# Gates of the merge ahead of its projections, a head in 128-row pieces behind products of zeros, and a last output block in halves

## The chip, the cores and the metric

The kernel runs on one core of a Trainium2 chip. The metric is the device time of one execution in microseconds (us), as a median of repeated runs. Before the change it is 2555.0 us (2554.29 to 2555.2 in 3 runs). One further execution was profiled; all times of single instructions come from it.

## The reference

One block of a hybrid network on 256 tokens with 2048 features, in fp32: a gated feed-forward layer, a mixer with two recurrent branches, cross-attention over a memory of 256 tokens, a second feed-forward layer, and a last norm.

```python
h = rmsnorm(x, norm_ffn1)
x = x + 0.5 * ((silu(h @ w1) * (h @ w3)) @ w2)
h = rmsnorm(x, norm_mix)
(mq, mk, mv, mo, mi, mf, hq, hf, hi, hg, gate_m, gate_h) = split(h @ w_in)
y_m = mlstm_mixer(mq, mk, mv, mo, mi, mf, ...)      # 4 heads
y_h = hgrn2_mixer(hq, hf, hi, hg, ...)              # 8 heads
merged = sigmoid(gate_m) * (y_m @ w_proj_m) + sigmoid(gate_h) * (y_h @ w_proj_h)
x = x + merged @ w_out
x = x + cross_attention(rmsnorm(x), rmsnorm(mem), w_q, w_kv, w_o)
x = x + 0.5 * swiglu(rmsnorm(x), ...)
return rmsnorm(x, norm_final)
```

## The kernel before

**Products.** Every large product goes through `gemm_nat`. It makes a block of 2 x 128 tokens by 512 columns (344 for three of the mixer's), in two PSUM banks `pa`. The activations stand still and the weights stream. Each fp32 operand is split into a high and a low part (activations `oh`, `ol`; weights `wh`, `wl`), and for each 128 rows of weights and each token half three products are made: high x high (L248), high x low (L249), low x high (L250). Weights come in units of 512 rows (1 MB, tile `wr`, four buffers, DMAs on SP). Each unit is worked off in two steps called subs, of 2 x 128 rows and 12 products each. For each sub ScalarE (ACT) makes `wh` by a cast and VectorE (DVE) makes `wl` by a subtraction, three subs ahead of the products (`SPLIT_AHEAD`).

**Order of the work.** `self.steps` is one list of subs and functions for the whole block, and `run` goes through it. After each sub `tick` adds the sub's modelled duration to a clock `self.pe`. Pieces of other work wait in two lists: `timed` (after so many ticks) and `bg` (in order). `tick` issues pieces while the modelled end of DVE's and ACT's queues, kept by `Paced` from a base and a price per element, is less than `BACKLOG` = 2.0 us ahead. All engines take their queues in order; within limits the framework's scheduler also reorders independent instructions when the program is built. `written(p)` runs timed pieces until an operand that a product needs has been issued; `flush` empties both lists.

**The head.** `load_x` (L425) orders the DMAs on SP: two halves of the first quarter of x, the first unit of weights in two halves, then quarters of x and units in turn. `first` transposes the first quarter on TensorE (PE), eight 128x128 pieces into two banks (L277), and splits them with the norm's gain. The first sub follows.

**The mixer and its merge.** The recurrent branches' work stands in `bg`: `hgrn_levels`, `hgrn_out`, `mlstm_weights`, `mlstm_scores`, `mlstm_out`. Their results are transposed by DVE in 16 steps of 32x256 (`tt<-mo`) into operand pairs `self.Y`. The merge loops over four column blocks c: gate `gm`, gate `gh`, `y_h @ w_proj_h`, `y_m @ w_proj_m`. After the gates of c = 0 stands a `flush()`.

**The end.** The last block (c = 3 of the second `w2`) runs with `late=4`: the products of token half 1 of its last 8 x 128 rows are put behind those of half 0, so that half 0 is finished, normed and written meanwhile. `done_last` then does for each half: add to x, squares on ACT, sum, `rstd` on GpSimd (POOL, L447), product with the gain, scaling, four DMAs.

Of the kernel before, what the change touches and what calls it, by code (L numbers as in the profile page):

```python
# [19 lines left out]
P = 128  # L20
# [79 lines left out]
class Core:  # L100
    def __init__(self, nc):
        self.tensor, self.gpsimd, self.sync = nc.tensor, nc.gpsimd, nc.sync
        self.vector, self.scalar = Paced(nc.vector, 0.13, 0.00106), Paced(nc.scalar, 0.22, 0.00082)


class Block:
# [74 lines left out]

    def flush(self):
        while self.timed or self.bg:
            if self.timed:
                self.next_timed()
            else:
                self.bg.popleft()()
# [9 lines left out]
    def split(self, s):  # L197
# [8 lines left out]
        self.nc.scalar.copy(s.hi, raw)  # L206
        self.nc.vector.tensor_sub(s.lo, raw, s.hi.bitcast(F32))
# [17 lines left out]


    def gemm_nat(self, ops, wap, n0, n, evac, kts=None, row0=0, late=0):
# [6 lines left out]
        def mm_for(k0, nk):  # L234
            def mm(hi, lo, ts=(0, 1)):
                if k0 == 0:
                    box["ps"] = [self.pacc([P, n]) for _ in range(2)]
                if k0 >= nkt - 2 * late and len(ts) == 2:
                    ts = (0,)
                    box.setdefault("late", []).append(lambda: mm(hi, lo, (1,)))  # L240
                for j in range(nk):
                    kt = k0 + j
                    xh, xl = self.written(pairs[kt // 4])
                    for t in ts:
# [5 lines left out]
                        nc.tensor.matmul(o, a_l, hi[:, j, :], start=False, stop=(kt == nkt - 1))  # L250
            return mm

        for k0 in range(0, nkt, 4):
            u = Unit(wap, row0 + k0 * P, 4, n0, n, 2)
            for q in range(2):
                self.steps.append(Sub(u, q, mm_for(k0 + 2 * q, 2)))
# [4 lines left out]
        def finish():  # L261
# [3 lines left out]
            evac(box["ps"], (1,))  # L265
        self.do(finish)

    def turn(self, src, gain, dst, halves=(0, 1)):
# [3 lines left out]
        for h in halves:  # L272
            ps = self.ps([P, 2, T])
            for j in range(2):
                for t in range(2):
                    c = (2 * h + j) * P
                    nc.tensor.transpose(ps[:, j, t * P:(t + 1) * P], src(t)[:, c:c + P], self.ident)  # L277
# [3 lines left out]
            else:  # L281
                for j in range(2):
                    k = 2 * h + j
                    g = gain[:, k:k + 1]
                    nc.scalar.activation(hi[:, k, :], ps[:, j, :], AF.Copy, scale=g)
                    nc.vector.scalar_tensor_tensor(
                        lo[:, k, :], in0=ps[:, j, :], scalar=g, in1=hi[:, k, :].bitcast(F32),
                        op0=ALU.mult, op1=ALU.subtract)
            if h == 1:
                self.unwritten.pop(id(dst), None)  # L290

# [5 lines left out]
    def written(self, p):  # L297

        while id(p) in self.unwritten:
            self.next_timed()  # L300
        return p
# [44 lines left out]
    def setup(self):  # L346
# [21 lines left out]
        def load(group):  # L368
            st = self.const.tile([P, P], F32, name=self.nm("stage"))
            first = group[0][1]  # L370
            for name, o, n in group:
# [3 lines left out]
                nc.scalar.dma_start(st[o - first:o - first + n, :], src.rearrange("(k p) -> k p", p=P))  # L375
# [8 lines left out]

        nc.scalar.dma_start(self.ident, a["consts"][:, :P])
        turn_first = load(groups[0])
        nc.vector.memset(self.mhalf, -0.5)

        def rest():
            nc.scalar.dma_start(c[:, P:], a["consts"][:, P:])  # L390
            turns = [load(g) for g in groups[1:]]
            self.gbias = self.const.tile([P, 8], F32, name="gbias")
            nc.scalar.dma_start(self.gbias[:, 0:4], a["mlstm_ig_bias"][0].partition_broadcast(P))
            nc.scalar.dma_start(self.gbias[:, 4:8], a["mlstm_fg_bias"][0].partition_broadcast(P))
# [8 lines left out]
        return turn_first  # L403

# [37 lines left out]
    def rstd_of(self, ss, n, dim):  # L442
# [4 lines left out]
        nc.gpsimd.tensor_tensor(r, ms, self.mhalf[:, :n], op=ALU.pow)  # L447
        return r

    def squares(self, src, ss_col):  # L450
        junk = self.t2([P, 512], name="junk")
        self.nc.scalar.activation(junk[:, :src.shape[-1]], src, AF.Square, accum_out=ss_col)
# [22 lines left out]
    def squares_of(self, n, c):  # L475
        for t in range(2):
            self.squares(self.x[c][:, t, :], n.ss[:, t, c:c + 1])
# [17 lines left out]
    def ffn(self, norm, w1, w3, w2, chunk_done, end=False):  # L495
        nc = self.nc
        ops = LazyOps(lambda: norm().ops)
        for f0, f1 in ((0, 6), (6, 11)):
            us = [None] * (f1 - f0)
            for f in range(f0, f1):  # L500
# [16 lines left out]
                self.gemm_nat(ops, w1, f * 512, 512, evac_a)  # L517
                self.gemm_nat(ops, w3, f * 512, 512, evac_b)
            for c in range(4):
                last = f1 == 11  # L520

                def evac(ps, ts=(0, 1), c=c, last=last):
# [7 lines left out]
    def mixer(self, norm, chunk_done):  # L530
# [83 lines left out]
        merged = [None] * 4  # L614
        G = {}
        for c in range(4):
# [560 lines left out]
```

## Time and profile before

| | us |
|---|---|
| median of 3 runs | 2555.0 |
| the profiled execution, time of the run | 2555.04 |
| its span, first to last instruction | 2553.2 |
| outside the span | 1.84 |
| first PE instruction | 4.84 |
| first large product | 10.00 |
| last large product starts | 2544.05 |

Page part 1 gives the busy time of each engine; matmuls overlap in it, so that a busy PE says little. What counts is the step from one product to the next: the rows of the timeline show a product as 0.39 us long, but the next one starts 0.23 us later. The waits name what PE stood still for. The gates of c = 0 begin about 1090 us into the span.

### The profile page before, as it was taken

How to read it: one execution, taken by the hardware profiler on the slowest of the kernel's cores; microseconds unless marked ns; L12 is line 12 of the kernel's file. 1: busy time of each engine (PE TensorE's matmuls, PEld its weight loads, DVE VectorE, ACT ScalarE, POOL GpSimd, SP SyncE). 2: the span in 40 equal slices, each digit the busy share in tenths (PEclk: the TensorE clock that was granted, in tenths of full speed). 3: DMA queues.
4: the chain of work that ended last, by engine and by line, in shares of the span. 5: the costliest groups of instructions: out<-in, count | busy, mean ns of one | idle time of the engine just before them, and what ended most of it. 6: DMA issues, size and time to landing. Idle time of an engine off the chain costs nothing.

```text
span 2553.2 us, 29044 instructions
## 1 busy us (share of the span) xinstructions
PE 2528.8 (99%) x11431; PEld 2104.7 (82%) x11431; DVE 1730.7 (68%) x2384; ACT 1201.8 (47%) x1385; POOL 13.5 (1%) x21
## 2 busy tenths in 40 slices
PE   8999999999999999999999999999999999999998
PEld 7888888888888898787888888888888888888887
DVE  5767644767768878967666787677767574457664
ACT  5444434444455565644444454444544443344443
POOL 0000000000000000000000000000000000000000
PEclk9999999999999999999999999999999999999999
DMA  7665565565555545545555565555566556555653
GB/s 262 197 193 189 195 198 190 189 198 190 193 190 185 176 138 165 183 163 181 190 191 197 187 212 180 170 175 173 190 198 190 191 196 197 188 192 194 214 189 128
DMA packets 243305, 479.92 MB, mean 188 GB/s; under 512 B 8008, under 2 KB 14432, under 8 KB 243168
## 3 DMA queue, kind: packets, MB, share of 16 engines
q1 hardware_dynamic: 242016, 476.15, 57.4%
q10 hardware_dynamic: 1152, 1.92, 0.2%
q8 instruction: 89, 1.46, 0.2%
q14 instruction: 48, 0.39, 0.0%
HBM read 475.94 MB, written 2.10 MB: 187 GB/s over the span
## 4 chain that ended last, share of the span: by engine, by line
PE 92%; DVE 6%; issue 1%; ACT 0%; DMA 0%; POOL 0%; SPq 0%; POOLq 0%; ACTq 0%
PE pa L250 30%; PE pa L248 30%; PE pa L249 30%; DVE wl L90 2%; DVE tt L90 2%; PE ps L726 1%; DVE ol L90 1%; DVE cv L90 0%; PE ps L277 0%; DMA x<-in_x 0%; PE ps L966 0%; PE ps L967 0%; PE ps L965 0%; POOL rstd L447 0%; ACT kn L90 0%
## 5 line engine op out<-in xcount | busy, mean ns | idle before, releaser
L90 DVE TENSOR_TENSOR wl<-wr,wh 128x1024 fp32r<-128x1024 f32 (+1 forms) x904 | 1094.2, 1213 | 721.6 <-ACT wh L90 715.0
L90 ACT CAST wh<-wr 128x1024 fp32r<-128x1024 f32 (+1 forms) x904 | 942.0, 1045 | 1141.9 <-PE pa L250 1091.3
L248 PE MATMUL pa<-wh,oh 128*128 128x512 f32 (+1 forms) x3616 | 1409.7, 390 | 7.0 <-ACT oh L90 4.4
L249 PE MATMUL pa<-wl,oh 128*128 128x512 f32 (+1 forms) x3616 | 1403.6, 388 | 2.3 <-DVE wl L90 2.3
L250 PE MATMUL pa<-wh,ol 128*128 128x512 f32 (+1 forms) x3616 | 1402.5, 388 | 0.2 <-DVE ol L90 0.2
L248 PEld LDWEIGHTS pa<-wh,oh 128*128 128x128 f32 x3616 | 680.0, 188 | 143.3 <-ACT oh L90 4.8
L249 PEld LDWEIGHTS pa<-wl,oh 128*128 128x128 f32 x3616 | 680.2, 188 | 141.1 <-DVE wl L90 5.5
L250 PEld LDWEIGHTS pa<-wh,ol 128*128 128x128 f32 x3616 | 679.7, 188 | 138.8 <-DVE ol L90 0.7
L90 DVE STREAM_TRANSPOSE tt<-sil 32x256 f32<-32x256 f32 x352 | 153.6, 436 | 6.8
L90 DVE STREAM_TRANSPOSE tt<-x 32x256 f32<-32x256 f32 x144 | 62.8, 436 | 2.8
L90 ACT CAST oh<-tt 128x1024 fp32r<-128x1024 f32 x29 | 30.6, 1054 | 39.7 <-DVE tt L90 39.7
L90 ACT ACT_TABLE_LOAD x34 | 43.6, 1283 | 10.1 <-DVE rs L90 3.1
L90 ACT ACTIVATE oh<-tt,cols 128x256 fp32r<-128x256 f32 x52 | 23.3, 500 | 47.7 <-DVE tt L90 47.7
L90 ACT ACTIVATE sil<-pa,rstd 128x512 f32<-128x512 f32 x44 | 29.8, 689 | 17.8 <-PE pa L250 17.7
L90 DVE TENSOR_TENSOR ol<-tt,oh 128x1024 fp32r<-128x1024 f32 x29 | 35.4, 1220 | 1.6 <-ACT oh L90 1.4
L90 DVE STREAM_TRANSPOSE tt<-kn 32x256 f32<-32x256 f32 x64 | 27.9, 436 | 5.6 <-ACT kn L90 4.5
L90 DVE SCALAR_TENSOR_TENSOR sil<-pa,rstd,sil 128x512 f32<-128x512 f32 x44 | 31.0, 743 | 0.0
L90 DVE STREAM_TRANSPOSE qt<-qn 32x256 f32<-32x256 f32 x64 | 27.9, 436 | 4.1 <-ACT qn L90 3.0
L90 ACT ACTIVATE oh<-ps,cols 128x256 fp32r<-128x256 f32 x44 | 20.3, 473 | 21.4 <-DVE ol L90 15.6
L90 DVE COPY_PREDICATED at<-cst,ps 128x128 f32<-128x128 int32 x80 | 22.8, 328 | 10.6 <-PE ps L726 10.0
L90 ACT ACTIVATE junk<-x 128x512 f32<-128x512 f32 x40 | 24.9, 625 | 7.6 <-DVE x L90 7.0
L90 DVE SCALAR_TENSOR_TENSOR ol<-ps,cols,oh 128x256 fp32r<-128x256 f32 x44 | 20.7, 480 | 10.8 <-ACT oh L90 10.5
(174 smaller groups left out, 649.4 us busy)
## 6 DMA issues: line engine op xcount, KB each, us to landing
wr<-in_ffn_w SPq DMA_DIRECT2D x263, 1024.0 KB, 5.2
wr<-in_w_in SPq DMA_DIRECT2D x80, 1024.0 KB, 5.1
wr<-in_xattn_wkv SPq DMA_DIRECT2D x32, 1024.0 KB, 5.4
wr<-in_w_out SPq DMA_DIRECT2D x16, 1024.0 KB, 5.1
wr<-in_xattn_wq SPq DMA_DIRECT2D x16, 1024.0 KB, 5.0
wr<-in_xattn_wo SPq DMA_DIRECT2D x16, 1024.0 KB, 5.1
wr<-in_w_in SPq DMA_DIRECT2D x12, 688.0 KB, 4.1
wr<-in_w_proj_h SPq DMA_DIRECT2D x8, 1024.0 KB, 5.0
```

The lines of the kernel that those rows point to most:

```text
L90: return fn(out, *args, **kw)
L248: nc.tensor.matmul(o, a_h, hi[:, j, :], start=(kt == 0), stop=False)
L249: nc.tensor.matmul(o, a_h, lo[:, j, :], start=False, stop=False)
L250: nc.tensor.matmul(o, a_l, hi[:, j, :], start=False, stop=(kt == nkt - 1))
L726: nc.tensor.matmul(ps[:, i, :], kt[:, g, j * P:(j + 1) * P], S["qc"][:, 2 * g + j, :], start=True, stop=True)
```

## The change

It has five parts.

1. **Merge.** The gates of c = 0, 1, 2 are made first, then the projections of c = 0, the gates of c = 3, and the projections of c = 1 to 3. There is no `flush()` any more: `written` now also waits for operands that don't exist yet and takes pieces from both lists as a product needs them.
2. **Pacing.** `Paced` has other prices (DVE 0.19 us and 0.00104 per element instead of 0.13 and 0.00106, ACT 0.25 and 0.00085 instead of 0.22 and 0.00082), and `rstd_of` adds 0.9 us to DVE's modelled queue.
3. **Moved from DVE to ACT:** `prep_f` of the hgrn branch (8 x 128x256), the diagonals `di` (8 x 128x128) and the copies into `r0`, `r1` in `mlstm_weights`.
4. **Head.** PE first multiplies a tile of zeros with itself nine times and, after the first piece's transposes, four times more (`warm`). The first quarter of x is transposed by 128-row pieces into banks of their own, and the first unit's weights are split by 128 rows (four subs instead of two), in a pinned order: operand piece, weight piece. Squares come later. The small parameter loads go through SP instead of ACT's queue.
5. **End.** The last sub of token half 1 is made in two halves of 256 columns in banks of their own. The rest is added to x and summed before; each half is added, squared and folded into the sum of squares. Five DMAs instead of four per token half.

```diff
+    def next_piece(self):
+        if self.timed:
+            self.next_timed()
+        else:
+            self.bg.popleft()()
...
+            def halves(hi, lo, h):
+
+                o = self.pacc([P, n // 2])
+                c = slice(h * n // 2, (h + 1) * n // 2)
...
-    def written(self, p):
-
-        while id(p) in self.unwritten:
-            self.next_timed()
-        return p
+    def written(self, ops, i):
+
+        while ops[i] is None or id(ops[i]) in self.unwritten:
+            self.next_piece()
+        return ops[i]
...
+    def warm(self, n):
+
+        ps = self.ps([P, P])
+        for _ in range(n):
+            self.nc.tensor.matmul(ps, self.warm_tile, self.warm_tile, start=True, stop=True)
...
-            if c == 0:
-                self.do(lambda: self.flush())
...
+        for c in range(3):
+            gates(c)
+        merge(0)
+        gates(3)
+        for c in range(1, 4):
+            merge(c)
...
-                nc.vector.tensor_scalar(f[:, i, :], f[:, i, :], self.oml[:, hd:hd + 1], self.lb[:, hd:hd + 1],
-                                        op0=ALU.mult, op1=ALU.add)
+                nc.scalar.activation(f[:, i, :], f[:, i, :], AF.Identity, scale=self.oml[:, hd:hd + 1],
+                                     bias=self.lb[:, hd:hd + 1])
...
-                nc.vector.tensor_scalar(di, self.ident, ig[t], None, op0=ALU.mult)
+                nc.scalar.activation(di, self.ident, AF.Copy, scale=ig[t])
...
+            self.warm(9)
             self.load_x()
...
+            first_subs = [st for st in self.steps if isinstance(st, Sub)][:4]
+            for k in range(4):
+                self.turn_piece(src(0), n.gain, n.ops[0], k, pin)
+                if k == 0:
+                    self.warm(4)
+                self.split(first_subs[k])
...
+                    for h in range(2):
+                        sl = slice(256 * h, 256 * h + 256)
+                        ps = rest(h)
+                        pin(nc.vector.scalar_tensor_tensor(xs[:, sl], in0=ps, scalar=0.5, in1=xs[:, sl],
+                                                           op0=ALU.mult, op1=ALU.add))
+                        q = self.sm(1, "ssh")
+                        self.squares(xs[:, sl], q)
+                        if h == 1:
+                            pin(nc.vector.tensor_mul(xs[:, 0:256], xs[:, 0:256], gf[c][:, 0:256]))
+                        pin(nc.vector.tensor_scalar(ms, q, 1.0 / D, ms, op0=ALU.mult, op1=ALU.add))
```

How the instructions stand, at three places. First PE's queue at the head, before: `stage` holds the norm's gain, `x_92` and `x_93` are the first two quarters of x, `pa` the two token halves of the first block.

```order
L381 MATMUL ps_117<-cst,stage_89 128x16
L277 MATMUL ps_120<-cst,x_92 128x128
L277 MATMUL ps_129<-cst,x_92 128x128
L277 MATMUL ps_120<-cst,x_92 128x128 x3
L277 MATMUL ps_129<-cst,x_92 128x128 x3
L248 MATMUL pa_156<-wh_140,oh_109 128x512
L248 MATMUL pa_157<-wh_140,oh_109 128x512
L277 MATMUL ps_170<-cst,x_93 128x128 x2
L249 MATMUL pa_156<-wl_141,oh_109 128x512
```

And with the change (`x_106`, `x_107` are the same quarters):

```order
L449 MATMUL ps_96<-warm_88 128x128 x9
L417 MATMUL ps_131<-cst,stage_91 128x16
L320 MATMUL ps_134<-cst,x_106 128x128 x2
L449 MATMUL ps_139<-warm_88 128x128 x4
L320 MATMUL ps_148<-cst,x_106 128x128 x2
L320 MATMUL ps_157<-cst,x_106 128x128 x2
L320 MATMUL ps_166<-cst,x_106 128x128 x2
L269 MATMUL pa_175<-wh_144,oh_123 128x512
L269 MATMUL pa_176<-wh_144,oh_123 128x512
L270 MATMUL pa_175<-wl_145,oh_123 128x512
```

The zero products stand ahead of all else, and the transposes of the second quarter have moved behind eleven products. Second, DVE's queue where the last of the four pairs of `self.Y` is made, before: `mo` is the mlstm branch's result, `tt` its transpose, `ol` the low part of the pair, `gh<-pa,gh` the evacuation of the first projection.

```order
L90 SCALAR_TENSOR_TENSOR mo_6840<-ps_8484,mrr_8499,mo_6840 128x256 x2
L90 STREAM_TRANSPOSE tt_8505<-mo_6840 32x2x4x32 x16
L90 TENSOR_TENSOR wl_8585<-wr_8443,wh_8584 128x1024
L90 TENSOR_TENSOR gh_8465<-pa_8534,gh_8465 128x512
L90 SCALAR_TENSOR_TENSOR ol_8504<-tt_8505,cols,oh_8503 128x256 x4
```

With the change:

```order
L90 SCALAR_TENSOR_TENSOR mo_6842<-ps_8933,mrr_8948,mo_6842 128x256 x2
L90 STREAM_TRANSPOSE tt_9009<-mo_6842 32x2x4x32 x2
L90 TENSOR_TENSOR wl_8976<-wr_8869,wh_8975 128x1024
L90 STREAM_TRANSPOSE tt_9009<-mo_6842 32x2x4x32 x5
L90 TENSOR_TENSOR wl_8994<-wr_8869,wh_8993 128x1024
L90 STREAM_TRANSPOSE tt_9009<-mo_6842 32x2x4x32 x5
L90 TENSOR_TENSOR wl_9017<-wr_8915,wh_9016 128x1024
L90 STREAM_TRANSPOSE tt_9009<-mo_6842 32x2x4x32 x4
L90 TENSOR_TENSOR wl_9037<-wr_8915,wh_9036 128x1024
L90 SCALAR_TENSOR_TENSOR ol_8992<-tt_9009,cols,oh_8991 128x256 x4
```

The sixteen transposes no longer stand in one row, and in the rows that follow these, seven weight splits stand between `ol_8992` and the evacuation `gh<-pa,gh` of the first projection, where there was none before. Third, DVE's queue at the end, before, for token half 1: `x_95` is the last quarter of x, `x_92` the first, `x_94` the third, `sst` and `ms` lead to `rstd`.

```order
L90 SCALAR_TENSOR_TENSOR x_95<-pa_18406,x_95 128x512
L90 TENSOR_REDUCE sst_18574<-ss_18034 128x1
L90 TENSOR_TENSOR x_95<-x_95,gf_17582 128x512
L90 TENSOR_SCALAR ms_18576<-sst_18574 128x1
L90 TENSOR_SCALAR x_92<-x_92,rstd_18578 128x512
L90 TENSOR_SCALAR x_94<-x_94,rstd_18578 128x512
```

With the change (`x_109`, `x_106`, `x_108` are the same quarters, `ssh` the squares of a half):

```order
L90 SCALAR_TENSOR_TENSOR x_109<-pa_18435,x_109 128x512
L90 SCALAR_TENSOR_TENSOR x_109<-pa_18600,x_109 128x256
L90 TENSOR_SCALAR sst_18597<-ssh_18608,sst_18597 128x1
L90 SCALAR_TENSOR_TENSOR x_109<-pa_18612,x_109 128x256
L90 TENSOR_TENSOR x_109<-x_109,gf_17611 128x256
L90 TENSOR_SCALAR sst_18597<-ssh_18620,sst_18597 128x1
L90 TENSOR_TENSOR x_109<-x_109,gf_17611 128x256
L90 TENSOR_SCALAR x_106<-x_106,rstd_18626 128x256 x2
```

The product with the gain that stood ahead of `ms` is cut in two, and its second half stands behind the last fold.

More of the change, by code (lines that the diff above doesn't have):

```diff
@@ L249, in mm @@
                         nc.tensor.matmul(o, a_h, lo[:, j, :], start=False, stop=False)
[L250 removed]
+                        nc.tensor.matmul(o, a_l, hi[:, j, :], start=False, stop=(kt == end - 1))
             return mm
         for k0 in range(0, nkt, 4):
[L254 to L256 removed]
+            ns = 4 if fine and k0 == 0 else 2
+            u = Unit(wap, row0 + k0 * P, 4, n0, n, ns)
+            for q in range(ns):
+                self.steps.append(Sub(u, q, mm_for(k0 + 4 // ns * q, 4 // ns)))
         if not late:
@@ L515, in evac_b @@
                     self.turn_on_vector(s, None, us[f - f0])
-                self.gemm_nat(ops, w1, f * 512, 512, evac_a)
+                self.gemm_nat(ops, w1, f * 512, 512, evac_a, fine=f == 0 and not end)
                 self.gemm_nat(ops, w3, f * 512, 512, evac_b)
@@ L611, in mixer, with gates @@
         self.do(lambda: self.bg.extend(self.mlstm_out(M, MV, MO)))
-        merged = [None] * 4
-        G = {}
-        for c in range(4):
+        merged, G = [None] * 4, {}
+        def gates(c):
             for key, base in (("gm", 7176), ("gh", 9224)):
```

153 lines of the change are left out of this document (98 added, 55 removed).

## The prediction

> **What bounds the kernel now.** I read the page first, then PE's waits, then the stages in which PE stands still.
>
> ```profile
> span 2553.2 us, 29044 instructions
> PE 2528.8 (99%) x11431; PEld 2104.7 (82%) x11431; DVE 1730.7 (68%) x2384; ACT 1201.8 (47%) x1385; POOL 13.5 (1%) x21
> ```
>
> PE has work in 99% of the span, so nothing off PE is worth anything by itself. Only what PE loses can be won. The stages, with the number of PE's matmuls in brackets:
>
> ```profile
> core 0: us, PE busy (x) PEld busy (x) DVE busy (x) ACT busy (x) POOL busy (x), PEclk, DMA share, GB/s
> 10.00:26.00 16.00, 15.58 (x65) 12.28 (x65) 10.57 (x17) 12.71 (x29) 0.00 (x0) 1.00 1.05 386
> 1010.00:1036.00 26.00, 23.71 (x99) 17.81 (x98) 25.15 (x52) 12.69 (x17) 0.00 (x0) 1.00 0.38 124
> 1145.00:1152.50 7.50, 3.08 (x15) 2.23 (x13) 7.26 (x17) 1.63 (x3) 0.00 (x0) 1.00 0.42 138
> 1152.50:1160.00 7.50, 7.26 (x17) 5.01 (x18) 6.89 (x11) 3.10 (x5) 0.00 (x0) 0.54 0.23 65
> 2400.00:2500.00 100.00, 100.00 (x443) 82.81 (x442) 63.55 (x72) 44.64 (x49) 0.00 (x0) 1.00 0.59 192
> ```
>
> The last row is the steady state: 443 products in 100 us, a step of 0.226 us each. This is the floor, and the change leaves the number of large products as it is. The other rows fall short of it in three places: the head, the mixer at 1010 to 1036 and the merge at 1145 to 1160. The fourth loss is the tail, after the last product. The waits name what PE waited for:
>
> ```profile
> PE ps L381 <- DMA stage<-in_norm_ffn: 4.8, 1, 4.8
> PE pa L248 <- ACT oh L90: 4.4, 1, 4.4
> PE pa L248 <- ACT wh L90: 2.6, 1, 2.6
> PE pa L249 <- DVE wl L90: 2.3, 5, 0.5
> ```
>
> **Part 1, the merge's `flush` (8.2 us).** PE, DVE and ACT around the longest wait:
>
> ```profile
> 1147.67 0.39 PE L250 MATMUL pa<-wh,ol 128*128 128x512 f32 x1
> 1152.48 0.68 PE L248 MATMUL pa<-wh,oh 128*128 128x512 f32 x1 [4.42 <-ACT oh L90]
> 1144.71 7.18 DVE L90 STREAM_TRANSPOSE tt<-mo 32x256 f32<-32x256 f32 x16
> 1151.91 1.23 DVE L90 TENSOR_TENSOR wl<-wr,wh 128x1024 fp32r<-128x1024 f32 x1
> ```
>
> `flush` puts all that is left of the mlstm branch into DVE's queue at once. PE reaches the second half of `y_m @ w_proj_m` while DVE still has sixteen transposes to do. It stands from 1147.67 to 1152.48: 4.81 less one step of 0.226, 4.6 us. Afterwards the granted clock is 0.54: 17 products fit into 7.5 us, where 33 would at the steady step; 16 x 0.226 = 3.6 us. Together 8.2 us. With the change 3 blocks of gates of 2 x 96 products stand ahead of the first projection, instead of one: 2 x 192 x 0.226 = 87 us more cover for work that was late by 5. In DVE's new queue seven weight splits, each for 12 products or 2.7 us, stand between the last pair and the first evacuation of a projection. So the wait goes, and the slow clock with it. I take 8.2. The lower bound is 0, if another operand is as late; the upper is 8.7, since the three products after the wait had small gaps too. What the longer life of six gate tiles could cost is the last rival.
>
> **Part 2, pacing and the pieces moved to ACT (3.1 us).** At 1010 to 1036 DVE is busy for 25.15 of 26 us and PE waits for `wl`, five times in all. One of these:
>
> ```profile
> 1019.63 0.39 PE L248 MATMUL pa<-wh,oh 128*128 128x512 f32 x1
> 1020.52 0.50 PE L249 MATMUL pa<-wl,oh 128*128 128x512 f32 x1 [0.50 <-DVE wl L90]
> ```
>
> The wait is shown as 0.50 but costs 0.89 - 0.226 = 0.66, for a product's record is 0.16 longer than its step. The five waits so cost 2.3 + 5 x 0.16 = 3.1 us. What leaves DVE:
>
> ```profile
> L90 DVE TENSOR_SCALAR f<-f,oml,lb 128x256 f32<-128x256 f32 x8 | 3.0, 414 | 0.0
> L90 DVE TENSOR_SCALAR di<-cst,gs 128x128 f32<-128x128 f32 x8 | 2.3, 282 | 0.1
> ```
>
> That is 5.3 us, ahead of the stretch or in it, and ACT, at 12.69 of 26 us, has room. The new prices also put fewer pieces between two weight splits: a 256-element transpose counts 0.40 us before and 0.46 now, and takes 7.18 / 16 = 0.45. The work that is pushed back goes under the gates, which now have 87 us more. I take all of the 3.1; bounds 0 (the same load, a little later) and 4.0 (small gaps beside the five). ACT's new pieces wait for DVE with weight casts behind them, and each cast is made three subs or 3 x 12 x 0.226 = 8.1 us ahead; a wait of a few us is hidden, a longer one is a rival below.
>
> **Part 3, the head (3.3 us).** PE and ACT there:
>
> ```profile
> 8.90 1.04 ACT L90 CAST wh<-wr 128x1024 fp32r<-128x1024 f32 x1 [0.99 <-DMA wr<-in_ffn_w]
> 10.00 1.22 PE L248 MATMUL pa<-wh,oh 128*128 128x512 f32 x2 [2.60 <-ACT wh L90]
> 11.97 0.78 PE L249 MATMUL pa<-wl,oh 128*128 128x512 f32 x1
> 14.25 0.63 PE L249 MATMUL pa<-wl,oh 128*128 128x512 f32 x1
> 14.68 0.63 PE L250 MATMUL pa<-wh,ol 128*128 128x512 f32 x1
> 15.96 0.41 PE L250 MATMUL pa<-wh,ol 128*128 128x512 f32 x1
> 19.19 0.60 PE L277 MATMUL ps<-cst,x 128*128 128x128 f32 x4
> ```
>
> The first half unit of weights is there at 8.90, and the change moves no DMA ahead of it. A cast of half the size takes some 0.6 instead of 1.04 (estimate from the 0.63 of the 128x512 square below), so the first product can start at 9.6 instead of 10.0. From 10.00 to 26.00 PE makes 49 products and 16 transposes. At full step that is 49 x 0.226 + 16 x 0.11 (from the four transposes at 19.19) = 12.8 us; 3.2 are lost, in the gap up to 11.97 and in steps of 0.43 up to 15.96, where the step changes to 0.23. (PEclk reads 1.00 there; the steps tell that it was half.) So 0.4 + 3.2 = 3.6 can be won. The pieces keep up: for each 128 rows DVE needs an operand piece and a weight piece, about 0.45 + 0.65, and PE 6 x 0.226 = 1.36. Only the first `wl` is late, by 0.3. That leaves 3.3, if the clock is full when the first product starts.
>
> The zero products are there for that. A plain fp32 128x128 product takes
>
> ```profile
> 893.18 0.89 PE ps L747 x8
> ```
>
> 0.22 us at full clock (four in 0.89) and 0.44 at half. Nine take 2 to 4 us from about 1.0 on, when DVE has made the zeros, and four more up to 1.8 after the first transposes. They end by about 8, ahead of 8.90; the idle PE of before is their cover, and if they overran they would cost 0.44 each. In this trace the clock rose 4.0 us after PE's work became dense (11.97 to 15.96). The Trainium skill (TensorE: Matmul & The Clock Gate, Part 1: The HAM clock gate) says that the clock is raised after one window of about 3.4 us of sustained activity, which runs freely; the 4.0 us agree with it. It also says (Part 4: PE-mode transpose) that transposes don't count as busy in the same way, and the transposes of this head raised nothing; if zero products counted as little, the term would be the one of the second rival. If the clock rises only 4.0 us after the first product, half of 4.0 is lost: 1.3. I take 3.3, bounds 1.3 and 3.6. The squares moved back and the loads on SP stand behind weights that are needed later; the load queue waits for buffers then, so I cost them at 0, and at 0.5 if one delays a unit.
>
> **Part 4, the end (0.7 us).** DVE, ACT, POOL and SP after the last product, which ends at 2544.05 + 0.39 = 2544.44:
>
> ```profile
> 2544.05 0.39 PE L250 MATMUL pa<-wh,ol 128*128 128x512 f32 x1
> 2544.48 0.69 DVE L90 SCALAR_TENSOR_TENSOR x<-pa,x 128x512 f32<-128x512 f32 x1 [1.59 <-PE pa L250]
> 2545.20 0.63 ACT L90 ACTIVATE junk<-x 128x512 f32<-128x512 f32 x1 [1.86 <-DVE x L90]
> 2546.03 0.68 DVE L90 TENSOR_TENSOR x<-x,gf 128x512 f32<-128x512 f32 x1
> 2546.63 0.15 DVE L90 TENSOR_SCALAR ms<-sst 128x1 f32<-128x1 f32 x1
> 2546.86 0.55 POOL L447 TENSOR_TENSOR rstd<-ms,mhalf 128x1 f32<-128x1 f32 x1 [4.89 <-DVE ms L90]
> 2547.44 0.88 DVE L90 TENSOR_SCALAR x<-x,rstd 128x512 f32<-128x512 f32 x2 [0.67 <-POOL rstd L447]
> 2547.96 1.80 SPq L1124 DMA_DIRECT2D out<-x  x4
> ```
>
> The first DMA of half 1 goes out 3.5 us after the last product. With the change, counted from S, the end of the products that are not halved: the big add to S + 0.7, the first half's add to 1.2, its square with the read of the sum to 1.7, the fold to 1.9, the second add to 2.4, square to 2.9, fold to 3.1, POOL with its way there to 3.8, a half scaling to 4.1. Prices of halves:
>
> ```profile
> L90 DVE SCALAR_TENSOR_TENSOR mo<-ps,mrr,mo 128x256 f32<-128x256 f32 x8 | 3.5, 480 | 0.1
> L90 ACT ACTIVATE junk<-ps 128x256 f32<-128x256 f32 x8 | 3.0, 382 | 0.7 <-PE ps L899 0.7
> ```
>
> The products of the two halves take S to S + 1.4, so the first DMA goes out 2.7 us after the last product, 0.8 sooner. The second half's add waits behind the fold of the first; that is why it isn't 1.5. One DMA more costs up to 1.80 / 4 = 0.45 if issues set the end, nothing if the bytes do. I take 0.7; bounds 0.3 and 1.3.
>
> **Sum.** 8.2 + 3.1 + 3.3 + 0.7 = 15.3 us. The profiled execution took 2555.04, the median of the runs is 2555.0. 2555.04 - 15.3 = 2539.7 us.
>
> **Rivals.** *Zeros don't raise the clock*: the head gives 1.3, the time is 2541.7. For it: the eight transposes at the head raised nothing. Against it: they lasted 2.4 us only and had gaps. *The merge still waits*: the pieces, taken as needed, still pile up ahead of the projections, DVE is late again and the clock falls; without the 8.2 the time is 2547.9. Against it: 87 us of cover and the splits in DVE's new queue. *ACT's new waits* (slower): the diagonals and `r0`, `r1` have one buffer each, so of four mlstm heads the later three wait on ACT for DVE and for PE's products of the head before, with casts queued behind. It decides when such a chain takes more than the 8.1 us of lead. If a gate tile that finds no buffer adds to it, each head can cost what the merge's wait costs now, 8.2: three give 24.6 on top, 2564.3. Against it: DVE and PE reach these pieces within one or two subs, 2.7 us each.
>
> **How the numbers follow.** Forecast 0.61, zeros 0.18, merge 0.13, ACT 0.03; 0.05 for more than I forecast, up to 18 us, where the small gaps go as well. Measurement tells 0.2%, 5.1 us, from no change. All cases but ACT's lie more than that below 2555; I give 0.02 to a mixture of the zeros' and the merge's that stops within it. Faster 0.95, same 0.02, slower 0.03. The range goes from 2536 (all upper bounds: 3.6 + 8.7 + 4.0 + 1.3 = 17.6, and some gaps) to 2546, which takes in the zeros' rival with part 2 failing (2544.8) and leaves out the merge's and ACT's.
>
> **What would show it.** Right: products 0.23 apart from 9.6 on, no wait for `oh` and hardly any for `wl` in PE's waits, no clock under 1.00 near the merge, first DMA of half 1 some 2.7 us after the last product. Wrong: steps of 0.43 after 9.6; a wait of several us ahead of a projection; ACT behind PE or DVE for over 8 us among the mlstm heads.

## The result and the profile after

| | before | after |
|---|---|---|
| median of 5 runs, us | 2554.39 (2553.87 to 2555.2) | 2537.68 (2537.33 to 2537.85) |
| profiled execution: time, span, us | 2555.04, 2553.2 | 2537.33, 2535.5 |

The changed kernel is faster: the ratio is 0.9934, with a 95% interval of 0.992 to 0.9947. The medians differ by 16.7 us, the two profiled spans by 17.7: the profiled execution of before lies 0.65 above its median, that of after 0.35 below. The busy times of after:

```profile
PE 2525.5 (100%) x11463; PEld 2106.1 (83%) x11463; DVE 1729.4 (68%) x2372; ACT 1209.6 (48%) x1415; POOL 14.5 (1%) x21
```

DVE is busy for 1729 us, as before. What changed is where PE stood still. The same stages as in the prediction (us, PE busy, with the number of its matmuls in brackets, and so on, then PEclk):

```profile
10.00:26.00 16.00, 16.00 (x84) 13.24 (x83) 10.37 (x16) 10.02 (x19) 0.00 (x0) 1.00 1.04 387
1010.00:1036.00 26.00, 26.00 (x124) 21.78 (x124) 23.61 (x42) 11.34 (x12) 1.01 (x1) 1.00 0.50 172
1145.00:1152.50 7.50, 7.50 (x37) 6.21 (x37) 4.72 (x13) 2.74 (x4) 0.00 (x0) 1.00 0.41 140
1152.50:1160.00 7.50, 7.50 (x35) 6.29 (x34) 4.21 (x11) 3.77 (x10) 0.69 (x1) 1.00 0.43 140
2400.00:2500.00 100.00, 100.00 (x443) 82.78 (x442) 60.02 (x66) 41.79 (x47) 0.00 (x0) 1.00 0.61 196
```

PE is full in all of them, at a clock of 1.00, and the steady state is what it was: 443 products in 100 us. PE's waits, all that are left:

```profile
PE ps L449 <- DVE mhalf L90: 1.1, 1, 1.1
PE pa L270 <- DVE wl L90: 0.2, 1, 0.2
```

The first is the wait of the zero products for DVE's memset at the very start. No wait for `oh` is left, and of those for `wl` only 0.2 us, at 30.94. (A product that is held up by less than 0.16 us, by which its record is longer than its step, shows no wait here.)

To see where the 17.7 us come from, I count PE's large products from the start (one of 512 columns is 1, one of 344 columns 344/512) and compare when the N-th begins in each trace. After the 2000th the head is paid for, after the 6000th the mixer, after the 10000th the attention. The columns in the middle are experiments that are told below:

```
start of product N, us (in brackets: sooner than before)
N        before     merge alone       merge + prices     part 2 undone      after
2000     469.70     469.21 (0.5)      469.71 (0.0)       465.90 (3.8)       465.62 (4.1)
6000     1434.15    1425.26 (8.9)     1421.36 (12.8)     1421.94 (12.2)     1417.24 (16.9)
10000    2373.26    2364.38 (8.9)     2359.86 (13.4)     2361.04 (12.2)     2355.72 (17.5)
```

So the head gave 4.1 us, the mixer 12.8, the attention 0.6, and what comes behind the last product 0.2.

**The merge.** DVE in after, at the last transposes of the second pair of `y_m`:

```profile
1201.82 1.79 DVE L90 STREAM_TRANSPOSE tt<-mo 32x256 f32<-32x256 f32 x4
1203.64 1.23 DVE L90 TENSOR_TENSOR wl<-wr,wh 128x1024 fp32r<-128x1024 f32 x1
1204.78 1.67 DVE L90 SCALAR_TENSOR_TENSOR ol<-tt,cols,oh 128x256 fp32r<-128x256 f32 x4
```

The sixteen transposes of this pair come in groups of at most five with other work between, where before they came in one block of 7.18 us. They are done at 1206.5, and the product that waited at 1152.48 before comes at 1226 now (by the count of products). The operand is 20 us early.

**The head.** PE and ACT in after, and the DMA of the later constants on SP's queue:

```profile
1.05 4.11 PE L449 MATMUL ps<-warm 128*128 128x128 f32 x18 [1.05 <-DVE mhalf L90]
5.26 0.73 PE L320 MATMUL ps<-cst,x 128*128 128x128 f32 x2
5.83 1.06 PE L449 MATMUL ps<-warm 128*128 128x128 f32 x8
6.97 0.62 ACT L90 CAST wh<-wr 128x512 fp32r<-128x512 f32 x1 [0.47 <-DMA wr<-in_ffn_w]
7.65 0.73 PE L269 MATMUL pa<-wh,oh 128*128 128x512 f32 x2
8.37 0.50 PE L270 MATMUL pa<-wl,oh 128*128 128x512 f32 x1
8.71 0.40 PE L271 MATMUL pa<-wh,ol 128*128 128x512 f32 x1
8.95 0.40 PE L270 MATMUL pa<-wl,oh 128*128 128x512 f32 x1
22.69 0.50 SPq L430 DMA_DIRECT2D cst<-in_consts  x1
```

A zero product is two instructions here: the nine take 18 x 0.23 = 4.1 us, 0.46 each, so the clock is half; the four later ones take 8 x 0.13, so it is full by 5.83, 1.8 us ahead of the first real product. From 8.71 on the steps are 0.24. And the first cast starts at 6.97 instead of 8.90, which I had not forecast: in before, ACT's queue had issued the 705 KB of later constants right at the start, beside the first weights:

```profile
1.65 0.44 ACTq L390 DMA_DIRECT2D cst<-in_consts  x1
```

**The end.** DVE, POOL, and SP's issues behind the last product, which ends at 2526.97:

```profile
2527.57 0.21 DVE L90 TENSOR_SCALAR sst<-ssh,sst 128x1 f32<-128x1 f32 x1 [0.58 <-ACT junk L90]
2527.70 0.41 DVE L90 SCALAR_TENSOR_TENSOR x<-pa,x 128x256 f32<-128x256 f32 x1
2528.98 0.66 POOL L1197 TENSOR_TENSOR rstd<-sst,mhalf 128x1 f32<-128x1 f32 x1 [4.43 <-DVE sst L90]
2524.97 7.39 SPq L1209 DMA_DIRECT2D out<-x  x10
```

The five issues of half 1 start at 2530.06, 2530.49, 2530.96, 2531.46 and 2531.96. The first is 3.1 us behind the last product (3.5 before), but the last is 5.0 behind it (4.9 before), since there is one more. From the end of the last product to the end of the span it is 8.6 us, and was 8.8.

### The profile page after: what moved, and what is told of

Same layout as the page of the kernel before. It is cut to its first block, busy times and chain, and to the rows that moved or that the text cites. A ratio compares the mean times of both kernels' runs of the same rounds, so it can differ in the third digit from the quotient of the medians.

```text
span 2535.5 us, 29137 instructions
## 1 busy us (share of the span) xinstructions
PE 2525.5 (100%) x11463; PEld 2106.1 (83%) x11463; DVE 1729.4 (68%) x2372; ACT 1209.6 (48%) x1415; POOL 14.5 (1%) x21
## 4 chain that ended last, share of the span: by engine, by line
PE 98%; DVE 0%; ACT 0%; issue 0%; DMA 0%; SPq 0%; POOLq 0%; POOL 0%; DVEq 0%; ACTq 0%
PE pa L270 32%; PE pa L269 32%; PE pa L271 32%; PE ps L783 1%; PE ps L1023 0%; PE ps L1024 0%; PE ps L1022 0%; PE ps L299 0%; DVE wl L90 0%; ACT wh L90 0%; DMA wr<-in_ffn_w 0%; ACT junk L90 0%; PE ps L1097 0%; DVE ol L90 0%; DVE x L90 0%
## 5 line engine op out<-in xcount | busy, mean ns | idle before, releaser
L90 DVE TENSOR_TENSOR wl<-wr,wh 128x1024 fp32r<-128x1024 f32 (+2 forms) x906 | 1093.8, 1211 | 701.7 <-ACT wh L90 694.2
L90 ACT CAST wh<-wr 128x1024 fp32r<-128x1024 f32 (+2 forms) x906 | 942.0, 1043 | 1121.8 <-PE pa L271 1075.6
L90 ACT ACTIVATE junk<-x 128x512 f32<-128x512 f32 (+1 forms) x41 | 25.0, 612 | 7.0 <-DVE x L90 7.0
```

What stands on the lines that cost most here:

```text
L90: return fn(out, *args, **kw)
```

## The experiments

The kernel before had medians of 2554.55 to 2554.9 us beside these runs. Times are compared with 2537.68, the median of after, which was not run again beside them, so that differences of under 0.5 us need the trace as well. "After" stands for the changed kernel.

**1. Without the zeros.**

```diff
-            self.warm(9)
...
-                if k == 0:
-                    self.warm(4)
```

> The changed kernel without its products of zeros; all else is as it was. Theory Z (the zeros raise the clock): the first product still starts at about 7.65, but the steps are 0.43 for some 4.0 us from there, as before the change; half of 4.0 is lost, and a little in the transposes ahead: 2537.7 + 2.0 to 2.6, 2539.7 to 2540.3 us. Rival N (the head's gain is all from an earlier first product, the clock would rise by the denser transposes anyway): steps of 0.23 from the first few products on, 2537.7 us, within 0.4.

Measured: 2539.21 us (2538.25 to 2539.33), 1.5 more. PE in the profiled execution, which is the 2538.25 one:

```profile
5.40 2.33 PE L320 MATMUL ps<-cst,x 128*128 128x128 f32 x8
7.97 1.22 PE L269 MATMUL pa<-wh,oh 128*128 128x512 f32 x2 [0.25 <-ACT wh L90]
8.99 0.63 PE L270 MATMUL pa<-wl,oh 128*128 128x512 f32 x1
9.79 0.39 PE L270 MATMUL pa<-wl,oh 128*128 128x512 f32 x1
10.02 0.40 PE L271 MATMUL pa<-wh,ol 128*128 128x512 f32 x1
```

The first products are at the half clock, as theory Z has it, and rival N falls: the time is 1.5 more, where it allowed 0.4. But theory Z is too large. The clock is full at 9.79 already, 1.8 us behind the first product, not 4.0: 4.4 us behind the first transposes, which now run into the products with a hole of 0.25 us only. The zeros are worth 0.9 in this execution, the shortest of the four, and 1.5 in the median, not 2.0.

**2. The later constants from ACT's queue again.**

```diff
-            nc.sync.dma_start(c[:, P:], a["consts"][:, P:])
-            turns = [load(g, nc.sync) for g in groups[1:]]
+            nc.scalar.dma_start(c[:, P:], a["consts"][:, P:])
+            turns = [load(g, nc.scalar) for g in groups[1:]]
```

The two DMAs of the gate biases go with them.

> The changed kernel with the later constants (705 KB), the gains and the gate biases loaded from ACT's queue again, as before the change. Theory L (the first weights came 1.9 us sooner because the 705 KB no longer share the memory with them): the first weight cast starts at about 8.9 again and the first product at about 9.6; the clock is full by then; 2537.7 + 1.9 = 2539.6 us. Rival P (the 128-row pieces alone made the first product earlier): the first cast stays within 0.3 of 6.97, 2537.7 us, within 0.4.

Measured: 2540.58 us (2539.81 to 2541.51), 2.9 more. ACT and PE in the profiled execution, the longest of the four:

```profile
9.10 0.62 ACT L90 CAST wh<-wr 128x512 fp32r<-128x512 f32 x1 [2.34 <-DMA wr<-in_ffn_w]
6.98 0.82 PE L320 MATMUL ps<-cst,x 128*128 128x128 f32 x6
9.77 0.73 PE L269 MATMUL pa<-wh,oh 128*128 128x512 f32 x2 [1.97 <-ACT wh L90]
11.27 0.63 PE L270 MATMUL pa<-wl,oh 128*128 128x512 f32 x1
11.70 0.63 PE L271 MATMUL pa<-wh,ol 128*128 128x512 f32 x1
14.69 0.39 PE L271 MATMUL pa<-wh,ol 128*128 128x512 f32 x1
```

The DMA is issued at 1.72, as it was before the change, and the cast is back at 9.10: theory L has the landing right. In this execution it cost more than its 1.9, since PE idles for 2.0 us from 7.80 on, and the clock, which had been full, is half from about 10.8 to 14. The 2000th product starts at 469.76 here and at 469.70 in before: nothing of the head's 4.1 us is left. Two of the four executions took 2539.8 us, 2.1 more than after and near theory L's 1.9; the other two, this one among them, took 2541.3 and 2541.5. Their mean granted clocks are 0.999 and 0.998, which fits a fall of the clock in the two longer ones only. The earlier landing is what the zeros need to be of use. The Trainium skill (DMA: Bandwidth & Descriptors, Queues, rings and completion order) says that each DMA engine goes round robin between the queues that have work for it; that 705 KB on ACT's queue delay a 512 KB load on SP's by 2 us agrees with it.

**3. The merge in the order of before, with the flush.**

```diff
-        for c in range(3):
-            gates(c)
-        merge(0)
-        gates(3)
-        for c in range(1, 4):
-            merge(c)
+        for c in range(4):
+            gates(c)
+            if c == 0:
+                self.do(lambda: self.flush())
+            merge(c)
```

> The changed kernel with the merge in the order of before: gates of one column block, the flush, then its projections. Theory M (the order and the flush cost the 8.2 us): PE waits 4 to 5 us for an operand of y_m ahead of a projection, then the clock falls for some 7 us; 2537.7 + 8.2 = 2545.9 us. Rival D (DVE, relieved by the new prices and the moved pieces, would be in time for the flush too): no wait over 1 us, 2537.7 to 2539 us.

Measured: 2549.78 us, 12.1 more. DVE, PE, and the stage behind the second wait, where the clock is 0.62:

```profile
1128.28 7.19 DVE L90 STREAM_TRANSPOSE tt<-mo 32x256 f32<-32x256 f32 x16
1147.50 7.18 DVE L90 STREAM_TRANSPOSE tt<-mo 32x256 f32<-32x256 f32 x16
1155.27 0.79 PE L269 MATMUL pa<-wh,oh 128*128 128x512 f32 x1 [4.69 <-ACT oh L90]
1156.00:1162.00 6.00, 6.00 (x19) 4.70 (x18) 2.65 (x5) 1.40 (x3) 0.00 (x0) 0.62 0.36 100
```

Theory M holds and is too small. Both pairs of `y_m` have their sixteen transposes in one block now, and PE waits for both, 6.6 us by the waits. Behind each the clock is half, 0.50 from 1136.8 to 1140.0 and from 1153.9 to 1160.5, which costs some 5 us more. The new prices push work back, and with the flush all of it piles up: the stall of 8.2 us has grown to 12.1, which eats most of what the prices bring (4.7, run 8). The parts are not independent; the prices need the order.

**4. The same order without the flush, operands on demand.** As run 3, but without the flush:

```diff
-        for c in range(3):
-            gates(c)
-        merge(0)
-        gates(3)
-        for c in range(1, 4):
-            merge(c)
+        for c in range(4):
+            gates(c)
+            merge(c)
```

> The changed kernel with the projections of a column block right behind its gates, as before the change, but without the flush: the operands are taken on demand. Theory C (the 87 us of cover by more gates ahead are what counts): the rest of the branch is queued one piece after the other when its operand is asked for, DVE is as late as with the flush; 2537.7 + 6 to 9 us, 2544 to 2547 us. Rival O (taking on demand is what counts, the queue is shorter when the operand is asked for): a wait of under 1 us, no lower clock, 2537.7 to 2539 us.

Measured: 2555.62 us, 17.9 more, and twice what theory C had; rival O falls. PE and DVE at the wait:

```profile
1136.24 0.59 PE L953 MATMUL ps<-v,ew 128*128 128x256 f32 x2
1138.68 7.18 DVE L90 STREAM_TRANSPOSE tt<-mo 32x256 f32<-32x256 f32 x16
1146.45 0.79 PE L269 MATMUL pa<-wh,oh 128*128 128x512 f32 x1 [9.62 <-ACT oh L90]
```

Without cover, taking on demand is worse than the flush: what is left is queued only when PE's next product needs it. From 1124.6 on PE has no large product, only the branch's own small ones up to L953, and then it stands for 9.6 us while DVE makes the sixteen transposes. All of PE's waits near the merge add to some 13 us, and the clock is half, 0.50, until 1153, which costs 3 more on the products behind 1146.45. The rest of the 17.9, some 1.4, is what these nine waits hide at 0.16 each (an estimate). What made part 1 work is the 87 us of gates ahead.

**5. The merge alone, on the kernel of before.** The new order, `written` on demand, no flush; nothing else:

```diff
-            if c == 0:
-                self.do(lambda: self.flush())
...
+        for c in range(3):
+            gates(c)
+        merge(0)
+        gates(3)
+        for c in range(1, 4):
+            merge(c)
...
-        while id(p) in self.unwritten:
-            self.next_timed()
+        while ops[i] is None or id(ops[i]) in self.unwritten:
+            self.next_piece()
```

> The kernel of before with the first part of the change alone: three blocks of gates first, no flush, operands on demand. Theory M (the order alone is worth the 8.2): 2554.4 - 8.2 = 2546.2 us, no wait of a microsecond or more near the merge, the five waits for a weight split at 1019 to 1034 still there. Rival (it needs the relief of DVE by the second part): 2550 us or more, with a wait ahead of the first projection of y_m.

Measured: 2546.36 us, 8.3 less than before in the same runs (2554.65), as theory M has it. PE is full at 1145 to 1160; DVE is as full as before at the mixer, and the five waits stay:

```profile
1010.00:1036.00 26.00, 23.67 (x99) 17.84 (x98) 25.18 (x52) 12.69 (x17) 0.00 (x0) 1.00 0.40 127
1152.50:1160.00 7.50, 7.50 (x35) 6.21 (x34) 7.29 (x12) 3.98 (x7) 0.00 (x0) 1.00 0.42 141
PE pa L252 <- DVE wl L90: 2.3, 5, 0.5
```

**6. Part 2 undone.** Old prices, and the forget gates, the diagonals and the two short copies on DVE again:

```diff
-        self.vector, self.scalar = Paced(nc.vector, 0.19, 0.00104), Paced(nc.scalar, 0.25, 0.00085)
+        self.vector, self.scalar = Paced(nc.vector, 0.13, 0.00106), Paced(nc.scalar, 0.22, 0.00082)
...
-        nc.vector.end += 0.9
...
-                nc.scalar.activation(di, self.ident, AF.Copy, scale=ig[t])
+                nc.vector.tensor_scalar(di, self.ident, ig[t], None, op0=ALU.mult)
```

> The changed kernel with the old prices, and the forget gates, the diagonals and the two short copies back on DVE: all of the second part undone. Both theories: the waits for a weight split at the mixer come back, five of 0.5 us or more by the waits, and the small gaps with them: 2537.7 + 3.1 to 5, 2540.8 to 2542.7 us. The difference to the run with the old prices alone is what the moved pieces are worth: over 2 us by rival A, under 1 us by theory R. If the time stays under 2539, the new order of the merge took the waits away, not the second part.

Measured: 2542.6 us, 4.9 more. The waits for `wl` are back:

```profile
PE pa L270 <- DVE wl L90: 2.5, 6, 0.5
```

**7. The old prices alone,** the pieces stay on ACT:

```diff
-        self.vector, self.scalar = Paced(nc.vector, 0.19, 0.00104), Paced(nc.scalar, 0.25, 0.00085)
+        self.vector, self.scalar = Paced(nc.vector, 0.13, 0.00106), Paced(nc.scalar, 0.22, 0.00082)
...
-        nc.vector.end += 0.9
```

> The changed kernel with the old prices of DVE's and ACT's work (0.13 + 0.00106 and 0.22 + 0.00082 us, and nothing for the way to POOL); the pieces moved to ACT stay there. Theory R (the new prices, which put fewer pieces between two weight splits, took the five waits for a weight split away): they come back in part, 2537.7 + 2 to 4 us, 2539.7 to 2541.7 us. Rival A (the pieces moved to ACT did it): no wait for a weight split at the mixer, 2537.7 to 2538.2 us.

Measured: 2549.08 us, 11.4 more, which neither theory had: it is 6.5 worse than with the pieces on DVE as well. DVE, ACT and PE at an mlstm head:

```profile
1041.38 1.80 DVE L90 STREAM_TRANSPOSE cv<-k 32x256 f32<-32x256 f32 x4
1043.63 0.40 ACT L90 ACTIVATE di<-cst,gs 128x128 f32<-128x128 f32 x1 [6.12 <-DVE r L90]
1043.60 0.49 PE L890 MATMUL ps<-r,cst 128*128 128x128 f32 x2 [1.68 <-DVE r L90]
1048.93 0.46 PE L887 MATMUL ps<-r,cst 128*128 128x129 f32 x2 [2.07 <-DVE r L90]
1051.05 0.49 PE L890 MATMUL ps<-r,cst 128*128 128x128 f32 x2 [1.04 <-DVE r L90]
1052.38 0.63 PE L269 MATMUL pa<-wh,oh 128*128 128x512 f32 x1
```

The waits for `wl` are back (2.3 us in five), as theory R has it; rival A falls. ACT does wait for DVE among the mlstm heads, as in the prediction's third rival: the diagonal has one buffer, and ACT stands for 6.1 us until DVE has used the last one. But that is less than the 8.1 us by which the casts run ahead, and DVE does not idle for a cast there. What PE waits for is `r`, which DVE makes: it stands in DVE's queue behind two splits and eight transposes, of which the last four are shown. PE waits for it three times, 4.8 us, and then has steps of 0.43 from 1051.96 to 1054.9. These two make the 6.5. With the pieces on DVE (run 6) PE has no wait for `r`. Why the same prices put `r` so late only when the diagonals are on ACT is not shown; DVE's modelled queue is shorter without them, so that more transposes may be issued ahead.

**8. The merge and the prices, on the kernel of before.** Run 5 with the new prices (without the 0.9 us for the way to POOL); the pieces stay on DVE:

```diff
-        self.vector, self.scalar = Paced(nc.vector, 0.13, 0.00106), Paced(nc.scalar, 0.22, 0.00082)
+        self.vector, self.scalar = Paced(nc.vector, 0.19, 0.00104), Paced(nc.scalar, 0.25, 0.00085)
```

> The kernel of before with the first part of the change and the new prices (without the 0.9 us for the way to POOL); the forget gates, the diagonals and the short copies stay on DVE. Undoing prices and pieces together cost 4.9 us, undoing the prices alone 11.4. If the prices alone bring the 4.9 (the pieces on ACT are worth nothing by themselves): 2546.4 - 4.9 = 2541.5 us, no wait for a weight split over 0.3 us at the mixer. If the pieces must leave DVE as well: 2544 to 2546.4 us, with waits for a weight split left.

Measured: 2541.68 us, 4.7 less than with the merge alone. PE is full at the mixer, and DVE has 4.4 us less to do there:

```profile
1010.00:1036.00 26.00, 26.00 (x128) 21.93 (x128) 20.77 (x38) 11.46 (x13) 2.01 (x2) 1.00 0.48 162
```

In the table above the mixer (from the 2000th product to the 6000th) gives 12.8 us here and 12.8 in after; the attention 0.6 and 0.6. The pieces on ACT, together with the 0.9 us for the way to POOL, are worth nothing that the traces show; the prices are worth all of part 2.

**9. The first weights in four DMAs.** Each has 256 KB:

```diff
-                self.load(units[c], parts=2 if c == 0 else 1)
+                self.load(units[c], parts=4 if c == 0 else 1)
```

> The changed kernel with the first unit of weights loaded in four DMAs of 256 KB instead of two of 512 KB. If the first product waits for the landing of its weights: the first 128 rows land up to 0.9 us sooner (256 KB at the 280 GB/s of that stretch), the cast can start at 6.5 behind the first operand piece, the first product comes at 7.2 instead of 7.65, 2537.2 us. If the pieces behind it set the pace (DVE's 1.16 us for each 128 rows): under 0.2 us, 2537.6 us.

Measured: 2537.68 us, the same. The first product comes at 7.05 instead of 7.65, so it did wait for the landing. But by the 50th product this trace is 0.1 behind after, and from the 100th on 0.4 (it is the longest of the four executions, 2538.08). ACT at the second unit of weights:

```profile
13.02 1.05 ACT L90 CAST wh<-wr 128x1024 fp32r<-128x1024 f32 x1 [0.65 <-DMA wr<-in_ffn_w]
```

The head start ends there: this cast waits for its weights, where in after it starts at 12.61 without a wait, and the casts behind it stay 0.4 late. The four DMAs bring the first rows sooner, but not the second unit; the memory delivers 390 GB/s from 10 to 20 us here and 388 in after.

**10. The second add ahead of the first fold.**

```diff
+                        qs.append(self.sm(1, "ssh"))
+                        self.squares(xs[:, sl], qs[h], pin=pin)
-                        if h == 1:
-                            pin(nc.vector.tensor_mul(xs[:, 0:256], xs[:, 0:256], gf[c][:, 0:256]))
-                        pin(nc.vector.tensor_scalar(ms, q, 1.0 / D, ms, op0=ALU.mult, op1=ALU.add))
+                    pin(nc.vector.tensor_scalar(ms, qs[0], 1.0 / D, ms, op0=ALU.mult, op1=ALU.add))
+                    pin(nc.vector.tensor_mul(xs[:, 0:256], xs[:, 0:256], gf[c][:, 0:256]))
+                    pin(nc.vector.tensor_scalar(ms, qs[1], 1.0 / D, ms, op0=ALU.mult, op1=ALU.add))
```

> The changed kernel with the end in another order on DVE: the second half's add right behind the first half's, and the folds of the squares behind both. Theory (the second add waits 0.7 us behind the first fold, which waits for ACT): the second add goes from 2527.70 to about 2527.0, the first output DMA of half 1 and the end come 0.4 to 0.6 us sooner; 2537.2 us. Rival (the issues of the five output DMAs set the end): also sooner by as much, since the issues start sooner; if the bytes set it, the end stays, 2537.7 us.

Measured: 2537.07 us (2536.82 to 2537.26), 0.6 less, the theory's. DVE and POOL:

```profile
2526.29 1.65 DVE L90 SCALAR_TENSOR_TENSOR x<-pa,x 128x512 f32<-128x512 f32 x3
2528.82 0.66 POOL L1198 TENSOR_TENSOR rstd<-sst,mhalf 128x1 f32<-128x1 f32 x1 [3.76 <-DVE sst L90]
```

The three adds run back to back. POOL starts 1.35 us behind the last product (which ends at 2527.47), against 2.0 in after. The rival of the issues has the same sign; this run does not tell the two apart, run 11 does.

**11. Two of the five output DMAs from ACT.**

```diff
-                    nc.sync.dma_start(self.out[0][t * P:(t + 1) * P, c2 * 512 + lo:c2 * 512 + hi], xs[:, lo:hi])
+                    q = nc.scalar if c2 % 2 else nc.sync
+                    q.dma_start(self.out[0][t * P:(t + 1) * P, c2 * 512 + lo:c2 * 512 + hi], xs[:, lo:hi])
```

> The changed kernel with two of the five output DMAs of each half issued by ACT instead of SP. Theory I (the issues, 0.48 us apart on SP, set the end, which is why one DMA more ate the sooner start): the last issue comes about 0.9 us sooner and the end 0.6 to 0.9 us, 2536.9 us. Rival B (the bytes of the last transfers set the end): within 0.2 us of 2537.7.

Measured: 2537.24 us (2537.15 to 2537.34), 0.4 less. ACT's issues:

```profile
2530.86 0.94 ACTq L1210 DMA_DIRECT2D out<-x  x2
```

The last issue, ACT's second, starts at 2531.46, 4.1 us behind the last product instead of 5.0. Theory I has the sign, but the end came by 0.4 only, half of what the issue gained. The Trainium skill (DMA: Bandwidth & Descriptors, Issuing engines are not separate DMA queues) says that issuing from several engines saves only the time that the sequencer takes to initiate them; that it saved 0.4 us here agrees.

**12. Both edits of the end,** the diffs of runs 10 and 11 together.

> Both edits of the end together: adds first, and two of five output DMAs on ACT. If the two add up: 0.5 + 0.8 = 1.3 us sooner than the changed kernel, 2536.4 us. If only one of them sets the end, 2536.9 to 2537.2 us.

Measured: 2536.59 us (2536.49 to 2536.61), 1.1 less than after: 0.6 and 0.4 add up. The span ends 7.5 us behind the last product, against 8.6. This is the fastest version; its ratio to before is 0.9929 (0.9917 to 0.9942).

## Why the prediction came out as it did

The forecast was 2539.7 us, the result 2537.68, inside the range, and two microseconds off because three of four terms were mis-sized. Two of them came out above their own upper bounds and one below its lower bound. That the time still lies inside the range is in part luck: it is 1.7 us from its end, in the room that I had left for small gaps. In the profiled executions:

| term | forecast (bounds) | measured | from |
|---|---|---|---|
| 1 merge | 8.2 (0 to 8.7) | 8.3 by medians, 8.4 by the table | run 5 |
| 2 pacing and pieces | 3.1 (0 to 4.0) | 4.7 by medians, 5.0 by the table | runs 6 and 8 |
| 3 head | 3.3 (1.3 to 3.6) | 4.1 | table |
| 4 end | 0.7 (0.3 to 1.3) | 0.2 | last product to the end |

**Part 1** was right in mechanism and size: the wait of 4.6 and the slow clock of 3.6 behind it are both gone. Run 4 adds what the prediction left open: it is the cover that does it, not the taking on demand.

**Part 2** had the right place and the wrong cause in half. I counted 5.3 us of pieces that leave DVE; run 8 shows that they bring nothing. The prices do it, by the way that I named second: fewer pieces between two splits, and the rest goes under the gates. The term was too small for two reasons. At the mixer 4.4 us came back, more than the five waits and my bound of 4.0, since small gaps went too. And I looked for no gain in the attention, where the same prices gave 0.6. What I priced as a remote rival, ACT's new waits at 0.03, shows in run 7 in another form: ACT waits, but by less than its lead, and PE waits for a piece of DVE's that the old prices put too late. Moved pieces need prices that keep DVE's queue short. It is 6.5 us there, not 24.6, since PE's waits added to 4.8 and the clock fell once.

**Part 3** failed in one step: "the change moves no DMA ahead of it". It moves one away from beside it. I costed the constants' DMA at 0 on SP's queue and did not ask what it had done on ACT's: it held up the first weights by 1.9 us (6.97 against 8.90). So the first product came 2.35 us sooner, 7.65 against 10.00, where I gave the start 0.4. The sum of the head is only 0.8 too low because what comes behind the start gave 1.7 instead of 2.9. The two errors partly cancel. 0.4 is lost in the first three steps (7.65 to 8.71 takes 1.06, three steps are 0.68), where DVE's `wl` is late; the forecast had 0.3 for that. The larger loss comes later: the lead over before is 5.1 at the 80th product and 4.15 at the 100th, and both kernels have made the same transposes by then. DVE and PE there:

```profile
29.66 1.22 DVE L90 TENSOR_TENSOR wl<-wr,wh 128x1024 fp32r<-128x1024 f32 x1 [1.68 <-ACT wh L90]
30.94 0.73 PE L270 MATMUL pa<-wl,oh 128*128 128x512 f32 x2 [0.15 <-DVE wl L90]
```

The split that PE needs at 30.94 waited for its cast, and on ACT that cast stands behind two squares (27.36 to 28.5). These are the squares that the change moved back and that I costed at 0: ACT had done all eight by 25.3 before, and does them from 23.0 to 35.9 now. A later split ends at 33.98, and the product that needs it starts 0.2 late, at 34.04. No run puts the squares back, so that their part in the 1.0 us is read from the order on ACT and not shown by an experiment. The zeros themselves are worth 0.9 to 1.5 us, where I took 2.0: I had the 4.0 us from the head of before, where PE had a hole of 2.6 us, and in the new head the transposes run into the products. The Trainium skill (TensorE: Matmul & The Clock Gate, Part 4: PE-mode transpose) says that transposes don't count as busy in the same way. Run 1 neither needs nor excludes that: its clock rose 4.4 us behind the first transpose, but only 1.8 behind the first product. The zeros did what they are for: the rival of zeros that raise nothing, which Part 3 of the prediction calls the second though it is listed first, is out, for their own step has halved by 5.83.

**Part 4** was forecast at 0.8 for a first DMA 2.7 us behind the last product; it is 3.1. The chain is the one that I forecast, but longer. The big add starts 0.2 late, since DVE still scales half 0, the first fold ends 2.2 us behind the last whole product instead of 1.9, POOL 4.1 instead of 3.8, and the first DMA goes out at 4.5 instead of 4.1. And I gave the fifth DMA "0.45 if issues set the end": they do, in part (run 11). The first issue is 0.4 sooner, the last is not, and the end is 0.2 sooner.

## What to carry to other kernels

When background work is put between the steps of a bound engine, what it costs in the model sets how much is queued ahead of the next operand; prices 15% too low for a 256-element piece (0.40 us for 0.46) cost 4.7 us here, while the pieces that were moved to another engine brought nothing. Work that is pushed back needs cover: the same prices that gave 4.7 us with the new order were nearly worthless in the old one, whose stall grew from 8.2 to 12.1. And a DMA that nobody waits for early is not free: on ACT's queue it held up the first weights on SP's by 2 us.

## What the runs showed of the hardware

The clock falls without a long idle stretch. In run 2 an idle of 2.0 us with small holes behind it brought it to half 3 us after the idle began; in run 7 waits of 1.7, 2.1 and 1.0 us within 9 us did. It seems not to fall each time: two of run 2's four executions were 1.5 us shorter than the other two, at a mean granted clock of 0.999 against 0.998. The Trainium skill (TensorE: Matmul & The Clock Gate, Part 1: The HAM clock gate) gives one idle window of about 3.4 us; here a window that was idle for about half was enough (an estimate from run 7: 0.7 + 1.0 of the 3.4 us ahead of the first slow step at 1051.6). These two falls lasted 3.1 to 3.4 us (granted clock 0.50 from 10.9 to 14.1 in run 2 and from 1051.8 to 1055.0 in run 7), in which half of the steps is lost, so that a wait of 2 us can cost 1.6 more. Behind the wait of 4.6 us in before it was half for longer (0.50 from 1152.7 to 1159.4). Zero products raise the clock as real ones do: 4.1 us of them at the half step, and the next ones at the full.
